# Sums of weight pieces made from DRAM to DRAM by copying and accumulating transfers, in a hybrid encoder layer

## The chip, the cores and the metric

The kernel runs on one core of a Trainium2 chip. The metric is the time of one execution in microseconds (us), measured on the device. A core has engines that run side by side: TensorE (PE in the profile; its weight loads are PEld), VectorE (DVE), ScalarE (ACT), GpSimd (POOL) and SyncE (SP). SP, ACT and POOL issue the transfers (DMA), which 16 DMA engines carry out.

## The reference, cut to what matters

One layer of an encoder with a model width of 1024 in float32, on 1056 frames in two request groups: 1024 of a prompt and 32 of a sample.

```python
h = rms_norm(x, g_mix); z = h @ w_in            # q, k, v, conv h/B/C, gates a/b: 50 columns of 128
a  = window_attention(q, k, v, sink) @ w_attn_out
bo = (cb * causal_conv3(cc * ch)) @ w_conv_out
x += (sigmoid(ga) * a + sigmoid(gb) * bo) @ w_mix_out
x += memory_attention(rms_norm(x, g_cross)) @ w_co
x += square(relu(rms_norm(x, g_mlp) @ w_up)) @ w_down       # 1024 -> 4096 -> 1024
y  = rms_norm(x, g_final)
```

The new keys and values, the last rows of the convolution and the memory keys and values are outputs too.

## The kernel before, in words

The 1056 frames lie in three chunks of 384, 384 and 288, with features on the partitions. Each matrix product is made from weight pieces of 128 x 1024 (512 KB). Every operand is split into a high part (cast on ACT, the helper's line L120) and a low part (the remainder, on DVE, L121), and each product is made of three matmuls: high x high, high x low, low x high.

Some products use fewer multiplications, by sums of operands (a Strassen-like scheme over 2 x 2 blocks): the *x pairs* (15 pairs of columns of w_in), the *up pairs* (12 pairs of columns of w_up) and the down product. They need sums of weight pieces as well as of activations. Where these are made is what the change is about:

- **Down.** For each of 8 (j, t) the four pieces s0..s3 of w_down give d3 = s2 + s3, d2 = s0 + s2, d0 = s0 + d3 and d1 = s1 + d0. The kernel before makes them on POOL, in 32 smaller steps: a load of 512 KB on POOL's own queue (L742), four additions of 128 x 256 (L749), a store of 512 KB into the DRAM tensor `wsum_d` (L750). The steps stand at chosen slots of the attention (13), in most x pairs (12) and, for the rest, among the last columns of w_in and the first of the attention's output. The down stage then loads w_sum pieces from `wsum_d` just as it loads w_down. In both tensors one 128 x 1024 piece is four runs of 256 numbers, so rows of 1 KB.
- **Pairs.** For columns r1 and r2 of a pair, halves a and b, `pair_sums` makes s31 = (r1a + r2a, r2a + r2b) and s24 = (r1a + s31b, r1b + s24a) from the two tiles in SBUF, 128 x 512 each: for an x pair two on DVE and two on POOL, for an up pair all four on POOL (L881 to L884). ACT and DVE split the result for the matmuls.

The stages follow each other in time: start with keys and values; 48 slots of attention units, with the projections of q, convolution and gates among them as other work; the start of the x pairs; the x pairs; the last columns of w_in and the attention's output; the convolution's output, mix and memory attention; the first columns of w_up; the up pairs; down; final norm. In each attention unit POOL normalises three of four heads (`S`, L579) with the reciprocal from DVE, ahead of TensorE's transposes (L589).

A scheduler orders the instructions of each engine from a simulation of their times, and `pin` keeps those that it is put around in the order of the program. A weight tile `wr` has two buffers. Loads of weights, activations and spilled tensors go on SP's queue, in order; POOL's transfers go on a queue of software descriptors.

In the start, the first weight is loaded in two halves on ACT's queue (L282, L283), behind the parameters, while SP loads the activations x0 in four parts (L290); TensorE runs 14 matmuls on a tile of ones (L328) before the data come.

## Time and profile before

| | us |
|---|---|
| median of 3 runs (lowest to highest) | 1767.47 (1766.37 to 1769.14) |
| the profiled execution | 1767.74 |
| its span, first to last instruction | 1766.0 |
| TensorE busy | 1733.7 |
| VectorE busy | 1213.3 |
| ScalarE busy | 846.1 |
| GpSimd busy | 657.9 |

The time of an execution is its span and 1.74 us around it. Busy time is time in which an engine carries out instructions; issuing of transfers does not count. The share of TensorE is 98% over the whole run, but what an edit is worth depends on the stage it is in, so the prediction goes by stages. In views of the trace a row `out<-in` names the tile written and the tile read, by the names of the program with their numbers left out.

### The profile page before, as it was taken

What the parts mean: (1) busy time and instruction counts of PE and PEld (TensorE: products, weight loads), DVE (VectorE), ACT (ScalarE), POOL (GpSimd) and SP (SyncE); (2) the same over time, 40 slices, a digit from 0 to 9 for tenths busy, and PEclk for the clock granted to TensorE, in tenths of its full rate; (3) what the DMA queues carried; (4) which work ended last, traced back from release to release, by engine and by line L of the source; (5) the groups of instructions that cost most, each with busy time, mean ns of one, the idle gap of its engine ahead of it and who ended that gap; (6) DMA issues with size and microseconds to landing.
All of it is one profiled execution on the core that took longest, in us unless ns stands there. A gap on an engine that the chain in (4) does not pass through costs nothing.

```text
span 1766.0 us, 30039 instructions
## 1 busy us (share of the span) xinstructions
PE 1733.7 (98%) x11008; PEld 1711.6 (97%) x11008; DVE 1213.3 (69%) x2130; ACT 846.1 (48%) x1625; POOL 657.9 (37%) x702
## 2 busy tenths in 40 slices
PE   8999999999999999999999999999999999999997
PEld 8999999999999999999999999999999999999997
DVE  6768888777887767367576877666666675445665
ACT  8667767852232245144465755642222353432553
POOL 2246675643744534402324241375544300100111
PEclk9999999999999999999999999999999999999998
DMA  5413434442322527789766767744443497544674
GB/s 183 146 58 106 141 114 147 139 153 98 132 86 96 177 102 263 261 255 320 259 218 208 242 219 240 253 166 155 130 139 124 149 316 221 176 152 141 230 240 134
DMA packets 178115, 313.01 MB, mean 177 GB/s; under 512 B 18192, under 2 KB 137776, under 8 KB 177840
## 3 DMA queue, kind: packets, MB, share of 16 engines
q1 hardware_dynamic: 168320, 276.97, 47.2%
q0 software_dynamic: 9216, 33.56, 5.4%
q8 instruction: 86, 1.41, 0.3%
q10 hardware_dynamic: 432, 0.58, 0.1%
q14 instruction: 61, 0.50, 0.1%
HBM read 233.23 MB, written 77.81 MB: 176 GB/s over the span
## 4 chain that ended last, share of the span: by engine, by line
PE 72%; DMA 9%; DVE 6%; ACT 5%; issue 3%; POOL 2%; SPq 1%; POOLq 0%; DVEq 0%; ACTq 0%
PE acc L176 7%; PE acc L178 7%; PE acc L177 7%; PE acc L892 7%; PE acc L894 7%; PE acc L893 7%; PE acc L1707 5%; PE acc L1706 5%; PE acc L1708 5%; PE pa L177 3%; PE pa L178 3%; PE pa L176 3%; DVE wl L121 2%; ACT wh L120 1%; PE pt L589 1%
## 5 line engine op out<-in xcount | busy, mean ns | idle before, releaser
L120 ACT CAST wh<-wr 128x1024 fp32r<-128x1024 f32 (+1 forms) x224 | 234.1, 1045 | 311.4 <-PE acc L1707 77.1
L121 DVE TENSOR_TENSOR wl<-wr,wh 128x1024 fp32r<-128x1024 f32 (+1 forms) x224 | 307.3, 1372 | 93.2 <-ACT wh L120 91.7
L176 PE MATMUL acc<-Y,wh 128*128 128x384 f32 (+1 forms) x624 | 201.9, 324 | 2.6 <-DVE ct L1081 1.5
L178 PE MATMUL acc<-Y,wl 128*128 128x384 f32 (+1 forms) x624 | 201.6, 323 | 0.3 <-DVE wl L121 0.3
L177 PE MATMUL acc<-Y,wh 128*128 128x384 f32 (+1 forms) x624 | 201.6, 324 | 0.0
L253 POOL TENSOR_TENSOR xacc<-xacc,ct 128x384 f32<-128x384 f32 (+1 forms) x62 | 78.0, 1257 | 322.2 <-ACT ct L251 319.8
L176 PE MATMUL acc<-X,wh 128*128 128x384 f32 (+1 forms) x528 | 172.6, 327 | 1.2 <-ACT wh L120 1.2
L177 PE MATMUL acc<-X,wh 128*128 128x384 f32 (+1 forms) x528 | 171.8, 325 | 0.9 <-DVE X L257 0.9
L178 PE MATMUL acc<-X,wl 128*128 128x384 f32 (+1 forms) x528 | 171.0, 324 | 0.0
L176 PEld LDWEIGHTS acc<-Y,wh 128*128 128x128 f32 x624 | 117.0, 188 | 3.9 <-DVE ct L1081 1.9
L178 PEld LDWEIGHTS acc<-Y,wl 128*128 128x128 f32 x624 | 117.2, 188 | 0.6 <-DVE wl L121 0.6
L177 PEld LDWEIGHTS acc<-Y,wh 128*128 128x128 f32 x624 | 117.1, 188 | 0.0
L579 POOL TENSOR_SCALAR S<-S,rec 128x256 f32<-128x256 f32 (+1 forms) x96 | 93.3, 984 | 62.1 <-DVE rec L576 61.9
L1706 PE MATMUL acc<-Y,wh 128*128 128x384 f32 (+1 forms) x352 | 113.1, 321 | 0.2 <-ACT Y L120 0.2
L1707 PE MATMUL acc<-Y,wh 128*128 128x384 f32 (+1 forms) x352 | 113.1, 321 | 0.1
L1708 PE MATMUL acc<-Y,wl 128*128 128x384 f32 (+1 forms) x352 | 112.9, 321 | 0.0
L120 ACT CAST wh<-s 128x1024 fp32r<-128x1024 f32 x54 | 56.6, 1051 | 105.9 <-PE acc L893 72.3
L177 PEld LDWEIGHTS acc<-X,wh 128*128 128x128 f32 x528 | 100.0, 189 | 2.9 <-DVE X L257 1.8
L176 PEld LDWEIGHTS acc<-X,wh 128*128 128x128 f32 x528 | 99.8, 189 | 2.2 <-ACT wh L120 1.4
L178 PEld LDWEIGHTS acc<-X,wl 128*128 128x128 f32 x528 | 99.8, 189 | 1.0 <-DVE wl L121 0.2
L121 DVE TENSOR_TENSOR Y<-ct,Y 128x384 fp32r<-128x384 f32 (+1 forms) x128 | 68.9, 570 | 28.7 <-ACT Y L120 28.5
L120 ACT CAST Y<-ct 128x384 fp32r<-128x384 f32 (+1 forms) x128 | 59.2, 486 | 60.0 <-DMA ct<-bc_d 14.8
(405 smaller groups left out, 5360.3 us busy)
## 6 DMA issues: line engine op xcount, KB each, us to landing
wr<-in_w_in SPq DMA_DIRECT2D x55, 512.0 KB, 3.6
wr<-in_w_up SPq DMA_DIRECT2D x48, 512.0 KB, 3.8
wr<-in_w_down SPq DMA_DIRECT2D x32, 512.0 KB, 4.0
wr<-wsum_d SPq DMA_DIRECT2D x32, 512.0 KB, 3.5
wl<-wl_d SPq DMA_DIRECT2D x28, 512.0 KB, 4.8
wr<-in_w_conv_out SPq DMA_DIRECT2D x24, 512.0 KB, 4.5
wr<-in_w_mix SPq DMA_DIRECT2D x24, 512.0 KB, 4.7
xacc<-in_w_down POOLq DMA_DIRECT2D x21, 512.0 KB, 3.9
```

The costliest lines, as they stand in the source:

```text
L120: act.copy(hi, src)
L121: dve.tensor_sub(lo, src, hi.bitcast(F32))
L176: pe.matmul(out, wh[:, a], hi, start=(k == 0), stop=False)
L177: pe.matmul(out, wh[:, a], lo, start=False, stop=False)
L178: pe.matmul(out, wl[:, a], hi, start=False, stop=(k == len(acts) - 1))
L579: pool_e.tensor_scalar_mul(stl[:, h, :nk], stl[:, h, :nk], rec[:, h : h + 1])
L892: pe.matmul(acc, wh[:, a], hi, start=(start and k == 0), stop=False, skip_group_check=True)
L893: pe.matmul(acc, wh[:, a], lo, start=False, stop=False, skip_group_check=True)
L894: pe.matmul(acc, wl[:, a], hi, start=False, stop=(k == 3), skip_group_check=True)
L1706: pe.matmul(a, wh[:, s], hi, start=(start and k == 0), stop=False, skip_group_check=True)
L1707: pe.matmul(a, wh[:, s], lo, start=False, stop=False, skip_group_check=True)
L1708: pe.matmul(a, wl[:, s], hi, start=False, stop=(stop and k == len(acts) - 1), skip_group_check=True)
```

## The change

Three parts.

**1. Down sums.** The pieces of w_down are laid out on the host as [q, j, t, 128, 1024], so that each is one block with rows of 4 KB, and `wsum_d` becomes four tensors of the same shape. Nothing of the sums passes through SBUF any more. For each (j, t), SP issues four DRAM-to-DRAM copies of 512 KB (d3 from s3, d2 from s0, d0 from s0, d1 from s1), and POOL issues five accumulating transfers of 512 KB in three phases: d3 += s2 and d2 += s2; d0 += d3 and d1 += d3; d1 += s0. One copy goes out in each attention slot from slot 2 (32 in all), one add in each from slot 8 (40 in all), with the phases of three (j, t) interleaved. The buffer `ws` and POOL's additions are gone.

**2. Up sums.** The same for the up pairs, two at a time, into four DRAM tensors `usum_d`: 24 copies on SP (three in each x pair from the second) and 30 adds on POOL (up to four in each x pair from the third). In the up stage each pair loads s31 and s24 with four transfers of 256 KB on SP, right behind the loads of the pair's own columns; `pair_sums` is left to the x pairs.

**3. Start.** The halves of the first weight are issued by SP, behind the first and second part of x0; the matmuls on ones become 18.

```diff
-    wsum_d = dram.tile([4, 2, 4, P, 4, 256], F32, name="wsum_d")
+    usum_d = [[dram.tile([12, P, 512], F32, name=f"us{k}{h}_d") for h in "ab"] for k in ("31", "24")]
+    wsum_d = [dram.tile([4, 2, P, 1024], F32, name=f"wsum_d{q}") for q in range(4)]
...
-            act.dma_start(raw[:, halves[0]], weight(worder[0])[:, halves[0]])
-            act.dma_start(raw[:, halves[1]], weight(worder[0])[:, halves[1]])
+            return [lambda h=h: sp.dma_start(raw[:, h], weight(worder[0])[:, h]) for h in halves]
...
                     sp.dma_start(raw[:, 2 * h : 2 * h + 2], io[f"x{c}"][:, 2 * h : 2 * h + 2])
+                    if first:
+                        first.pop(0)()
...
-        for _ in range(14):
+        for _ in range(18):
...
-            for to, x, y in ((3, 2, 3), (2, 0, 2), (0, 0, 3), (1, 1, 0)):
-                pin(pool_e.tensor_tensor(t[:, to], t[:, x], t[:, y], op=ALU.add))
-            pin(pool_e.dma_start(wsum_d[at], t))
...
+    def sum_parts(j, t):
+        s = [io["w_down"][q, j, t] for q in range(4)]
+        d = [wsum_d[q][j, t] for q in range(4)]
+        copies = [lambda to=to, x=x: pin(sp.dma_start(to, x)) for to, x in ((d[3], s[3]), (d[2], s[0]), (d[0], s[0]), (d[1], s[1]))]
+
+        def add(to, x):
+            return lambda: pin(pool_e.dma_start(to, x, accum_op=ALU.add, max_dma_last_dim=4096))
+
+        return copies, [[add(d[3], s[2]), add(d[2], s[2])], [add(d[0], d[3]), add(d[1], d[3])], [add(d[1], s[0])]]
+
+    sums = [sum_parts(j, t) for j in range(4) for t in range(2)]
+    copies = [x for c, _ in sums for x in c]
+    adds = [x for s in range(len(sums) + 2) for ph in (2, 1, 0) if 0 <= s - ph < len(sums) for x in sums[s - ph][1][ph]]
...
+    for i, x in enumerate(copies):
+        at(2 + i, x)
+    for i, x in enumerate(adds):
+        at(8 + i, x)
...
-        side = dve if key[0] == "x" else pool_e
-        side.tensor_tensor(s31[:, b], r2[:, a], r2[:, b], op=ALU.add)
+        dve.tensor_tensor(s31[:, b], r2[:, a], r2[:, b], op=ALU.add)
...
+        return [copy(s31b, r2b), copy(s31a, r1a), copy(s24a, r1a), copy(s24b, r1b)], [
+            [add(s31b, r2a), add(s31a, r2a)], [add(s24a, s31b), add(s24b, s31b)], [add(s24b, r1a)]
+        ]
...
+            if i and what in ("W1", "W4", "W3"):
+                for x in ucopies[:1]:
+                    ucopies.pop(0)()
+            if i > 1 and what in ("B11", "H", "W1", "W2"):
+                for x in uadds[:1]:
+                    uadds.pop(0)()
...
+    def up_sums(i):
+        if i >= len(UP):
+            return
+        for two, tag in zip(usum_d, ("s31", "s24")):
+            t = PW["pool"].tile([P, 1024], F32, tag=tag, name=nm(tag))
+            for h in range(2):
+                sp.dma_start(t[:, 512 * h : 512 * h + 512], two[h][i])
+            raws["u", i].append(t)
```

How the change stands in the order of the engines. First POOL in the attention, before: `xacc` and `ws` hold pieces of w_down, `S` are scores.

```order
L742 DMA xacc_2304<-in_w_down 128x1024
L749 TENSOR_TENSOR ws_2079<-ws_2079 128x256
L563 COPY S_2416<-nsink 128x4
L749 TENSOR_TENSOR ws_2079<-ws_2079 128x256 x3
L750 DMA wsum_d<-ws_2079 128x1024
L579 TENSOR_SCALAR S_2416<-S_2416,rec_2428 128x256 x3
L563 COPY S_2505<-nsink 128x4
```

The same place now; a transfer into `wsum_d` on POOL is an accumulating one:

```order
L737 DMA wsum_d_102<-in_w_down 128x1024
L737 DMA wsum_d_101<-wsum_d_104 128x1024
L578 TENSOR_SCALAR S_2425<-S_2425,rec_2437 128x256 x3
L737 DMA wsum_d_102<-wsum_d_104 128x1024
L562 COPY S_2516<-nsink 128x4
```

The load, the four additions and the store are gone, and single adds stand between the normalisations of the scores.

Then SP at the first stores of the attention's output (`m_d`), before: `ct` on the right are products, `wr` weights.

```order
L1082 DMA m_d_83<-ct_8400 128x384
L138 DMA wr_8623<-in_w_attn_out 128x1024
L1082 DMA m_d_84<-ct_8435 128x384
L1082 DMA m_d_83<-ct_8469 128x384
L1082 DMA m_d_84<-ct_8502 128x384
L1082 DMA m_d_85<-ct_8530 128x288
```

Now, with loads of x (`xt`) and of the memory keys (`mkr`):

```order
L1157 DMA xt_9560<-in_x 128x384
L1090 DMA m_d_83<-ct_8321 128x384
L1157 DMA xt_9602<-in_x 128x384
L1157 DMA xt_9644<-in_x 128x384
L1172 DMA mkr_9935<-mk_d 64x256 x2
L1090 DMA m_d_84<-ct_8349 128x384
L138 DMA wr_8532<-in_w_attn_out 128x1024
L1090 DMA m_d_83<-ct_8383 128x384
L1172 DMA mkr_9942<-mk_d 64x256 x2
```

The loads of x and of the keys, which came some 15 rows further down, stand among the first stores.

Last, POOL at the second up pair, before: `s` are the pair's sums, `xacc` the square of a half, `ct` a partial sum.

```order
L1424 TENSOR_TENSOR xacc_9241<-xacc_9241 128x384
L881 TENSOR_TENSOR s_2746_14009<-wr_2714_13769 128x512
L884 TENSOR_TENSOR s_2746_14009<-wr_13768,wr_2714_13769 128x512
L1356 TENSOR_TENSOR ct_13961<-ct_13959 128x288
L882 TENSOR_TENSOR s_2747_14010<-wr_13768,s_2746_14009 128x512
L1424 TENSOR_TENSOR xacc_9241<-xacc_9241 128x384
L883 TENSOR_TENSOR s_2747_14010<-wr_13768,s_2747_14010 128x512
```

Now:

```order
L1392 TENSOR_TENSOR Y_2665_13597<-lt_13575,Y_2664_13596 128x384
L1363 TENSOR_TENSOR ct_13875<-ct_13873 128x288
L1363 TENSOR_TENSOR ct_13920<-ct_13918 128x288
L1440 TENSOR_TENSOR xacc_9149<-xacc_9149 128x384
L1487 TENSOR_TENSOR lt_13988<-xacc_9149,lt_13988 128x384
```

The sums are gone from POOL; the rows around them follow each other directly.

More of the change, by code (lines that the diff above doesn't have):

```diff
@@ L126, in weight @@
             q, j, t = at
-            return (wsum_d if name == "w_sum" else io[name])[j, t, :, :, q].rearrange("i p c -> p i c")
+            return wsum_d[q][j, t] if name == "w_sum" else io[name][q, j, t]
         src = io[name]
@@ L136, in fetch_w @@
         raw = wp.tile([P, 1024], F32, tag="wr", bufs=2, name=nm("wr"))
[L137 to L138 removed]
+        sp.dma_start(raw, weight(worder[wpos[0] + len(fetched)]))
         fetched.append(raw)
@@ L326, in norm_x @@
         turn = ps.tile([P, P], F32, tag="pt", bufs=2, name=nm("pt"))
-        for _ in range(14):
+        for _ in range(18):
             pe.matmul(turn, ones_r, ones_r, start=True, stop=True)
-        load_w()
+        first = load_w()
         with tc.manual_schedule(engines={mybir.EngineType.SP}):
-            load_x()
+            load_x(first)
         w_half = first_w()
@@ L729, in at @@
         events.setdefault(slot, []).append(fn)
-    W = {}
-    pieces = [(j, t, i) for j in range(4) for t in range(2) for i in range(4)]
-    def sum_load(acc):
-        W["acc"] = acc
-        if pieces:
-            at = pieces.pop(0)
-            if acc:
-                t = xacc_tile()[:, :1024].rearrange("p (q c) -> p q c", q=4)
-            else:
-                t = W["pool"].tile([P, 4, 256], F32, tag="ws", name=nm("ws"))
-            pin(pool_e.dma_start(t, io["w_down"][at]))
-            W["new"] = at, t
-    def sum_add(old):
-        if old:
-            at, t = old
-            for to, x, y in ((3, 2, 3), (2, 0, 2), (0, 0, 3), (1, 1, 0)):
-                pin(pool_e.tensor_tensor(t[:, to], t[:, x], t[:, y], op=ALU.add))
-            pin(pool_e.dma_start(wsum_d[at], t))
-    def sum_step():
-        old = W.pop("new", None)
-        sum_load(not W.get("acc", True))
-        sum_add(old)
-    def sum_done():
-        sum_add(W.pop("new", None))
+    def sum_parts(j, t):
[8 more added lines that the diff above has]
+    adds = [x for s in range(len(sums) + 2) for ph in (2, 1, 0) if 0 <= s - ph < len(sums) for x in sums[s - ph][1][ph]]
     for kv, starts in enumerate([(0, 1, 2, 4, 5, 6, 8, 9, 10)] * 3 + [(0, 1, 2, 3, 4, 5, 6, 7, 8)]):
@@ L879, in pair_sums @@
         s24 = PW["pool"].tile([P, 1024], F32, tag="s24", name=nm("s24"))
-        side = dve if key[0] == "x" else pool_e
-        side.tensor_tensor(s31[:, b], r2[:, a], r2[:, b], op=ALU.add)
+        dve.tensor_tensor(s31[:, b], r2[:, a], r2[:, b], op=ALU.add)
         pool_e.tensor_tensor(s24[:, a], r1[:, a], s31[:, b], op=ALU.add)
         pool_e.tensor_tensor(s24[:, b], r1[:, b], s24[:, a], op=ALU.add)
-        side.tensor_tensor(s31[:, a], r1[:, a], r2[:, a], op=ALU.add)
+        dve.tensor_tensor(s31[:, a], r1[:, a], r2[:, a], op=ALU.add)
         raws[key] += [s31, s24]
@@ L905, in hybrid_step, with up_sum_parts, copy, add @@
     LATE = 3
+    def up_sum_parts(at):
+        g, i = at // 4 + 1, at % 4
+        r1, r2 = (io["w_up"][8 * g + i + e : 8 * g + i + e + 2] for e in (0, 4))
+        a, b = slice(0, 512), slice(512, 1024)
+        r1a, r1b, r2a, r2b = r1[:, :, a], r1[:, :, b], r2[:, :, a], r2[:, :, b]
+        (s31a, s31b), (s24a, s24b) = [[t[at : at + 2] for t in two] for two in usum_d]
+        flat = lambda t: t.rearrange("i p c -> (i p) c")
+        def copy(to, x):
+            return lambda: pin(sp.dma_start(flat(to), flat(x)))
+        def add(to, x):
+            return lambda: pin(pool_e.dma_start(flat(to), flat(x), accum_op=ALU.add, max_dma_last_dim=2048))
+        return [copy(s31b, r2b), copy(s31a, r1a), copy(s24a, r1a), copy(s24b, r1b)], [
+            [add(s31b, r2a), add(s31a, r2a)], [add(s24a, s31b), add(s24b, s31b)], [add(s24b, r1a)]
+        ]
+    usums = [up_sum_parts(at) for at in range(0, 12, 2)]
+    ucopies = [x for c, _ in usums for x in c]
+    uadds = [x for s in range(len(usums) + 2) for ph in (2, 1, 0) if 0 <= s - ph < len(usums) for x in usums[s - ph][1][ph]]
     xs1, xemit = {}, {}
@@ L993, in after @@
         def after(what):
-            if what == "B11":
-                sum_done()
             todo.get(what, lambda: None)()
-            if what == "W3" and (i % 5):
-                sum_load(True)
+            if i and what in ("W1", "W4", "W3"):
[4 more added lines that the diff above has]
+                    uadds.pop(0)()
             if what == "B11" and XP[i][0][0] == "a" and "cv_cm" in S:
@@ L1087, in do_attn_out @@
         return fn
+    item(lambda: [x() for x in ucopies + uadds])
     item(open_y)
@@ L1105, in hybrid_step @@
     run()
-    assert not pieces and "new" not in W
     todo.extend((bcp, bc_d, 1, k) for k in range(NF))
-    closed(W["cm"])
     closed(x_cm)
@@ L1620, in up_start @@
         up_issue(0, 3)
+        up_sums(1)
         A = up_p1(1)
```

28 lines of the change are left out of this document (10 added, 18 removed).

## The prediction

> **What bounds the kernel now.** I read the page's busy shares first, then the span cut by stages, then what TensorE waits for, then the chain of waits around the two waits that the change touches.
>
> The busy shares, share of the span and number of instructions:
>
> ```profile
> PE 1733.7 (98%) x11008; PEld 1711.6 (97%) x11008; DVE 1213.3 (69%) x2130; ACT 846.1 (48%) x1625; POOL 657.9 (37%) x702
> ```
>
> TensorE is busy 98% of the span. The change neither adds nor removes a matmul of the layer, so it can only win from the 1766.0 − 1733.7 = 32.3 us in which TensorE stands still, and it loses whatever it adds to them. The stages show where they lie. Columns: from and to, length, then busy us and instructions of each engine, granted TensorE clock, busy share of the 16 DMA engines, GB/s:
>
> ```profile
> 0.00:17.00 17.00, 11.34 (x51) 9.43 (x52) 10.87 (x17) 13.81 (x27) 4.25 (x10) 1.00 0.89 309
> 88.00:354.00 266.00, 265.93 (x1757) 257.90 (x1756) 210.94 (x576) 195.29 (x499) 168.43 (x228) 1.00 0.35 117
> 410.00:662.00 252.00, 252.00 (x1569) 252.00 (x1568) 189.68 (x255) 78.61 (x103) 119.55 (x131) 1.00 0.35 120
> 662.00:750.00 88.00, 86.31 (x545) 85.67 (x544) 51.79 (x71) 31.85 (x52) 39.19 (x51) 1.00 0.77 261
> 750.00:1165.00 415.00, 406.33 (x2572) 400.35 (x2572) 292.77 (x508) 232.33 (x434) 124.01 (x112) 1.00 0.74 249
> 1165.00:1400.00 235.00, 232.90 (x1457) 231.95 (x1456) 145.03 (x185) 62.70 (x81) 127.24 (x104) 1.00 0.40 132
> 1400.00:1501.00 101.00, 99.86 (x635) 98.34 (x634) 71.28 (x128) 44.08 (x82) 5.12 (x5) 1.00 0.78 254
> ```
>
> The attention slots (88 to 354) and the x pairs (410 to 662), where most of the old sums are made, have no idle TensorE at all: 0.07 and 0.00 us. There POOL's arithmetic is free, and removing it wins nothing. Idle time that the change can reach is the 1.69 us of attention's output (662 to 750), some of the 2.1 us of the up pairs (1165 to 1400), and the 1.14 us at the start of the down stage (1400 to 1501). TensorE's waits by line, us in total, times, longest:
>
> ```profile
> PE acc L176 <- DVE ct L1081: 1.5, 1, 1.5
> PE acc L892 <- ACT wh L120: 1.3, 1, 1.3
> PE acc L1708 <- DVE wl L121: 0.8, 1, 0.8
> PE acc L892 <- ACT s L1417: 0.2, 1, 0.2
> ```
>
> The first row is the idle time of 662 to 750; the second and the last lie between 1165 and 1185; the third is at 1472.
>
> **Attention's output (last pieces of the down sums, moved away).** The chain around 707 us (start, us, what), and the transfers of 686 to 710 (count, KB each, median us to landing; first two rows by queue: packets, MB, share of 16 engines):
>
> ```profile
> 698.34 6.28 DMA ct<-ao_d
> 706.09 1.90 DVE Y L121 x2
> 708.08 0.57 DVE ct L1081
> ```
>
> ```profile
> q1 hardware_dynamic: 3255, 5.68, 70.5%
> q0 software_dynamic: 576, 2.10, 23.8%
> ct<-ao_d SPq DMA_DIRECT2D x9, 192.0 KB, 6.1
> ws<-in_w_down POOLq DMA_DIRECT2D x1, 512.0 KB, 7.5
> ```
>
> DVE's last conversions of attention rows wait for a load that takes 6.28 us; DVE then does them before the product with the gate (ct, L1081) that frees an accumulator for TensorE. POOL's queue takes 23.8% of the DMA engines just then, all of it pieces of the down sums. Over the whole run the same 192 KB load takes less:
>
> ```profile
> ct<-ao_d SPq DMA_DIRECT2D x16, 192.0 KB, 4.4
> ```
>
> After the change these pieces are long done (their adds go out one per attention slot) and the last adds for the up weights leave POOL ahead of this stage. 94% busy engines (70.5 + 23.8) fall to about 70%, the load saves up to 6.28 − 4.4 = 1.9 us, and the 1.5 us wait goes with it. I take the whole idle time of the stage, **−1.7 us**. Its bounds: −1.7 (no more is idle here), and 0 if another load takes the place: the order hoists loads of the cross-attention keys and gates into these rows of SP's queue, among the output stores.
>
> **The up pairs' sums (48 POOL additions removed, 48 loads of 256 KB added).** The costliest of the four groups of additions in this stage (count, busy, mean ns, idle before), then the chain around 1181 us:
>
> ```profile
> L882 POOL TENSOR_TENSOR s<-wr,s 128x512 f32<-128x512 f32 x11 | 20.4, 1853 | 0.0
> ```
>
> ```profile
> 1174.67 1.25 POOL s L881
> 1175.92 1.25 POOL s L884
> 1177.79 1.24 POOL s L882
> 1179.78 1.28 POOL s L883
> 1181.09 1.05 ACT wh L120
> 1182.18 0.44 PE acc L892
> ```
>
> Four additions in a row, the cast of their result, and only then the matmul: this is the 1.3 us wait. With the sums loaded, the cast waits only for loads that the order puts ahead of the pair's first product. In the other pairs the additions (1.85 us each in the row above) are hidden: TensorE's products run on behind them, and of the 2.1 us idle in the whole stage only 2.1 − 1.5 = 0.6 are left for all of them. So the gain is 1.3 + 0.2 = **−1.5 us**, bounds −2.1 (all idle time of the stage) and 0 (the loads come late: 24 times 512 KB more in 235 us, at the 1.5 us of all engines worked out below, lift the DMA share from 0.40 to about 0.55).
>
> **Down weights in 4 KB rows.** The start of the down stage waits for a chain of transfers; its last member:
>
> ```profile
> 1475.96 4.05 DMA ct<-hid_d
> ```
>
> The row above for this stage has a DMA share of 0.78. Pieces of 1 KB become rows of 4 KB in the 64 weight loads of this stage. What rows of 4 KB are worth is seen only indirectly (KB, median us to landing):
>
> ```profile
> wr<-in_w_up SPq DMA_DIRECT2D x48, 512.0 KB, 3.8
> wr<-in_w_down SPq DMA_DIRECT2D x32, 512.0 KB, 4.0
> wr<-wsum_d SPq DMA_DIRECT2D x32, 512.0 KB, 3.5
> ```
>
> w_up has the 4 KB rows already, the others 1 KB pieces: no clear difference. The bounds are −1.1, all that is idle there, and 0; with no nearer row I take the middle, **−0.5 us**. The Trainium skill, page "DMA: Bandwidth & Descriptors", section "Specifications", gives 512 B as the smallest transfer for line rate; by it the term is 0, and the sum 3.2 us instead of 3.7. The three rows agree with it better than with a gain.
>
> **What is added in the attention and the x pairs.** 56 copies on SP's queue and 70 accumulating transfers on POOL's, 512 KB each. No row of before shows either. The nearest are POOL's own transfers of 512 KB, and the time they take of the 16 engines:
>
> ```profile
> q0 software_dynamic: 9216, 33.56, 5.4%
> xacc<-in_w_down POOLq DMA_DIRECT2D x21, 512.0 KB, 3.9
> wsum_d<-xacc POOLq DMA_DIRECT2D x21, 512.0 KB, 3.1
> ```
>
> 64 transfers take 5.4% of 1766, 95 us, so 1.5 us of all engines each. I take 1.5 for a copy (a load that ends elsewhere) and 1.5 to 3.0 for an add (one source read, or two). Attention, where 13 of the 32 old pieces lie: 32 × 1.5 + 40 × (1.5 to 3.0), less 26 old transfers × 1.5, is 69 to 129 us in the 282 of the attention slots; the share rises from 0.35 to 0.6 to 0.8. X pairs, with 12 old pieces: 24 × 1.5 + 30 × (1.5 to 3.0), less 24 × 1.5, is 45 to 90 in 252: 0.35 to 0.53 to 0.71. The stage from 750 to 1165 runs at 0.74, and its TensorE stands still 2%. The work in these two stages is cast and split well ahead, and TensorE is idle for 0.07 us in both together. POOL keeps in attention only the normalisation of the scores ahead of TensorE's transposes, and waits for it more than it works late:
>
> ```profile
> POOL S L579 <- DVE rec L576: 61.9, 23, 16.2
> ```
>
> That is a spare of 61.9/23 = 2.7 us each time, and the removed additions add to it. An add that needs an earlier add waits on POOL with the next normalisation behind it, but it goes out at least two slots after it, 2 × 5.9 us (the 48 slots fill this stage and some 16 us of the next, 282/48). Landing would have to exceed 11.8 us; load and store in a row take 3.9 + 3.1 = 7.0. I take **0**, bounds 0 and +10 (below). The 25 old pieces whose additions leave these stages win nothing, since nothing is idle there.
>
> **The start.** The first weight's halves go to SP's queue between the activations, and four warm-ups are added. The chain there:
>
> ```profile
> 4.86 0.61 ACT X L256
> 11.84 0.95 ACT wh L120
> 12.82 2.04 DVE wl L121
> 14.90 0.38 PE acc L188
> ```
>
> From 4.86 to 12.8 ACT works through its list; TensorE's last wait ends behind the split of the second weight. Bytes and their total are the same at 309 GB/s, so I take **0**; bounds −1 and +1 (an x part one transfer later).
>
> **Sum.** −1.7 − 1.5 − 0.5 + 0 + 0 = −3.7 us on the profiled execution, 1767.74 → 1764.0. That execution is 0.27 above the median of the runs, 1767.47, so I forecast **1763.8 us**. Its own range by the bounds of the four small terms is 1762 to 1768.
>
> **Rivals.**
> *The accumulates are slow, and POOL stands in their way (slower).* One mechanism: an add that waits for an earlier one holds POOL, the normalisation behind it is late, and TensorE's transposes (pt, L589) or the first x pair wait. It decides once an add lands after 11.8 + 2.7 = 14.5 us, twice the 7.0 above. Against it: the spacing. For it: transfers on busy engines do take twice as long (7.5 for a load of 3.9, rows above). At 16.5 us some 7 of the 40 adds would each cost 2 us: +14 − 3.7, or about 1777; at 15 us, 0.5 × 10 − 3.7: 1769. I price it at **1772**, chance 0.20. The Trainium skill, same page, section "Issuing engines are not separate DMA queues", says that transfers share the same 16 engines whichever engine starts them; the trace agrees, with SP's load at 6.1 beside POOL's at 7.5 in the window above, so moving sums off POOL does not take their bytes off SP's loads.
>
> *The stalls refill (same).* At 707 us the hoisted loads of keys and gates fill the place of the sums, so −1.7 falls away, or the sums' loads of the up pairs come late. Sum −2.0: **1765.5**, chance 0.33. For it: 64 KB keys took a place in SP's queue among the stores, and 70.5% of the engines stay busy; against it: they are small.
>
> *More is won (faster still).* With POOL's arithmetic gone, DVE and ACT run their splits earlier, and the whole idle time of 1400 to 1501 and part of the 8.7 us of 750 to 1165 go: −3.7 − 0.6 − 2.5, **1760.7**, chance 0.12. Against it: the POOL work that leaves lies before 750 and after 1165.
>
> **How the numbers follow.** The forecast has 0.35. A measurement of this kernel tells 0.2%, 3.5 us, from no change; the forecast lies just beyond it, at −3.7. Faster: most of the forecast's 0.35 that lies beyond −3.5 (0.22), the 0.12, and 0.08 for gains at several unpriced places, together 0.44; same: the 0.33 and the rest of the forecast, less what the tails take, 0.37; slower 0.19. The range that holds 8 in 10 leaves a tenth on each side: **1759 to 1774**.
>
> **What would show it.** The wait on ct L1081 near 707 us gone, and with it the ct<-ao_d landing near 4.4; no POOL s rows between 1165 and 1400, and no wait on wh L120 near 1181; POOL waiting for an accumulate less than 3 us at a time; no TensorE wait on L589 or L891-L893 new in attention or the x pairs. Wrong would be: DMA shares above 0.9 in attention, landing times of adds beyond 12 us, or a new wait in the first x pair.

## The result, and the profile after

The changed kernel takes **1793.82 us** (median of 4 runs, 1792.94 to 1800.18), the kernel before 1767.14 in the same comparison: a ratio of 1.0147, 95% interval 1.0131 to 1.0163. The forecast was 1763.8. It is 26.7 us slower, and outside the range of 1759 to 1774.

The profiled execution took 1793.94 us with a span of 1792.1. Its busy shares, and its stages cut at the same places of the work (some 10 to 27 us later on the clock than before):

```profile
PE 1741.6 (97%) x11012; PEld 1718.5 (96%) x11012; DVE 1166.2 (65%) x2130; ACT 844.0 (47%) x1625; POOL 491.3 (27%) x532
```

```profile
88.00:354.00 266.00, 264.02 (x1741) 255.99 (x1740) 202.60 (x572) 194.21 (x495) 139.99 (x186) 1.00 0.76 196
354.00:420.00 66.00, 60.99 (x375) 59.97 (x374) 45.33 (x66) 32.23 (x59) 25.20 (x25) 0.97 0.69 177
432.00:697.30 265.30, 249.08 (x1499) 246.65 (x1498) 161.53 (x244) 75.27 (x100) 86.74 (x96) 0.97 0.67 158
1180.00:1420.00 240.00, 238.47 (x1508) 237.91 (x1507) 138.41 (x191) 67.32 (x90) 71.56 (x64) 1.00 0.59 187
1420.00:1520.00 100.00, 97.93 (x620) 96.59 (x619) 70.83 (x128) 40.83 (x77) 5.07 (x5) 1.00 0.78 257
```

The third row holds 1499 matmuls of the x pairs. The same 1499 before:

```profile
426.90:668.00 241.10, 241.10 (x1499) 241.10 (x1498) 181.75 (x244) 76.82 (x100) 116.12 (x128) 1.00 0.34 115
```

So 24.2 us of the 26.7 are lost here: 16.2 in which TensorE stands still (265.3 − 249.1), and 8.0 because the same matmuls take longer (249.1 − 241.1). Up to 6.8 of these 8.0 come from the granted clock, 0.97 on average where it was 1.00 (worked out under "The clock" below). What TensorE waits for in this stretch now (before: nothing):

```profile
PE acc L877 <- DVE lt L980: 8.5, 3, 4.3
PE acc L877 <- DVE lt L972: 6.1, 3, 4.1
PE acc L877 <- ACT s L942: 1.6, 2, 1.1
```

These are the instructions with which DVE and ACT read a pair's products; they free the accumulators. They are late because POOL is. POOL's groups of accumulating transfers in this stretch, with the idle time of POOL just ahead of each (after the bar: busy us, mean ns, idle us and what ended it; on POOL the 0.9 us of issuing counts as busy):

```profile
L903 POOL DMA_DIRECT2D us31a_d<-in_w_up x6 | 5.4, 906 | 14.8 <-issue 14.8
L903 POOL DMA_DIRECT2D us24a_d<-us31b_d x6 | 5.4, 898 | 24.5 <-issue 24.5
L903 POOL DMA_DIRECT2D us24b_d<-in_w_up x6 | 5.4, 898 | 30.3 <-issue 27.4 <-DVE lt L980 3.0
L903 POOL DMA_DIRECT2D us24b_d<-us31b_d x6 | 5.4, 896 | 27.3 <-issue 27.3
L903 POOL DMA_DIRECT2D us31b_d<-in_w_up x5 | 4.5, 899 | 16.7 <-issue 8.2 <-DVE lt L966 5.5 <-DVE lt L973 3.0
```

POOL stands for 14.8 + 24.5 + 30.3 + 27.3 + 16.7 = 113.6 us ahead of 29 adds, and 102.2 of it are "issue": time in which it waits for nothing that the profile shows. One such place, first POOL, then ACT, DVE and TensorE behind it (start us, us, instruction, in brackets the idle time before it):

```profile
486.01 0.90 POOL L903 DMA_DIRECT2D us24b_d<-in_w_up  x1 [10.61 <-issue]
486.57 0.45 POOL L618 MEMSET u<- 128x2 f32 x1
486.61 1.18 POOL L619 COPY u<-prm 128x2 f32<-128x2 f32 x1
494.78 0.89 POOL L903 DMA_DIRECT2D us24a_d<-us31b_d  x1 [6.99 <-issue]
495.36 1.61 POOL L867 TENSOR_TENSOR s<-wr,s 128x512 f32<-128x512 f32 x1
497.05 1.29 POOL L868 TENSOR_TENSOR s<-wr,s 128x512 f32<-128x512 f32 x1
```

```profile
498.37 1.04 ACT L121 CAST wh<-s 128x1024 fp32r<-128x1024 f32 x1 [12.03 <-POOL s L868]
```

```profile
499.45 1.23 DVE L122 TENSOR_TENSOR wl<-s,wh 128x1024 fp32r<-128x1024 f32 x1 [10.33 <-ACT wh L121]
500.59 0.55 DVE L980 TENSOR_TENSOR lt<-acc,lt 128x384 f32<-128x384 f32 x1
```

```profile
501.29 0.42 PE L877 MATMUL acc<-tk,wh 128*128 128x384 f32 x1 [3.17 <-DVE lt L980]
```

Two adds hold POOL for 10.6 and 7.0 us, and the sums for the next x pair (L867, L868) stand behind them. ACT's cast waits 12 us for these sums and DVE's remainder 10 us for the cast. The instruction behind it on DVE, which frees the accumulator, is late with it, and TensorE stands for 3.2 us.

To see where time goes from stage to stage I matched the two executions matmul by matmul and took how much later each one starts (us; minus is earlier). The first column is the time in the kernel before; three kernels of the experiments below stand beside the change. Each column is one profiled execution.

```
at (before)                        change   down alone   4 KB rows   adds in x pairs
  23  start done                    -0.3       +0.1        +0.1          -0.5
 303  attention, most of it         -1.1       -0.8        -0.4          -1.7
 387  attention done                +0.4       +0.4        -1.3          -1.9
 407  x start done                  +5.1       +6.3        +3.9          +0.5
 688  x pairs done                 +29.2       +6.3        +3.9          +0.5
 749  attention's output            +27.0       +4.0        +1.6          -1.9
1132  memory attention done        +26.3       +1.9        -1.7          -4.4
1243  first up pairs               +26.9       +2.0        -0.7          -4.1
1705  down, most of it             +26.5       +3.2        +1.0          -3.6
```

The change loses 24.1 in the x pairs, 4.7 at the x start and 1.5 at the end of the attention, and gains 2.2 at the attention's output.

### The profile page after: what moved, and what is told of

Its sections match the earlier page's. It is cut to its first block, busy times and chain, and to the rows that moved or that the text cites. A ratio compares the mean times of both kernels' runs of the same rounds, so it can differ in the third digit from the quotient of the medians.

```text
span 1792.1 us, 30070 instructions
## 1 busy us (share of the span) xinstructions
PE 1741.6 (97%) x11012; PEld 1718.5 (96%) x11012; DVE 1166.2 (65%) x2130; ACT 844.0 (47%) x1625; POOL 491.3 (27%) x532
## 3 DMA queue, kind: packets, MB, share of 16 engines
q0 software_dynamic: 13920, 36.70, 12.5%
## 4 chain that ended last, share of the span: by engine, by line
PE 49%; DMA 5%; DVE 4%; ACT 2%; issue 1%; POOL 0%; SPq 0%; POOLq 0%; DVEq 0%; ACTq 0%
PE acc L176 5%; PE acc L177 5%; PE acc L178 5%; PE acc L1726 5%; PE acc L1724 5%; PE acc L1725 5%; PE acc L877 4%; PE acc L879 4%; PE acc L878 4%; DMA ct<-bc_d 2%; PE pa L177 1%; PE pa L176 1%; PE pa L178 1%; DVE wl L122 1%; DMA ct<-b_d 1%
## 5 line engine op out<-in xcount | busy, mean ns | idle before, releaser
L121 ACT CAST wh<-wr 128x1024 fp32r<-128x1024 f32 (+1 forms) x224 | 234.2, 1045 | 290.6 <-PE acc L1725 84.1
L122 DVE TENSOR_TENSOR wl<-wr,wh 128x1024 fp32r<-128x1024 f32 (+1 forms) x224 | 290.9, 1298 | 95.3 <-ACT wh L121 94.2
L121 ACT CAST wh<-s 128x1024 fp32r<-128x1024 f32 x54 | 56.2, 1049 | 126.6 <-PE acc L878 62.0
L122 DVE TENSOR_TENSOR wl<-s,wh 128x1024 fp32r<-128x1024 f32 x54 | 70.0, 1296 | 42.7 <-ACT wh L121 42.7
L877 PE MATMUL acc<-X,wh 128*128 128x384 f32 x240 | 82.4, 343 | 12.0 <-DVE lt L972 6.1
```

The lines of the kernel that those rows point to most:

```text
L121: act.copy(hi, src)
L122: dve.tensor_sub(lo, src, hi.bitcast(F32))
L877: pe.matmul(acc, wh[:, a], hi, start=(start and k == 0), stop=False, skip_group_check=True)
```

## The experiments

**Which part, and waits or traffic.** Four kernels. First the down sums alone: part 2 undone.

```diff
-        dve.tensor_tensor(s31[:, b], r2[:, a], r2[:, b], op=ALU.add)
+        side = dve if key[0] == "x" else pool_e
+        side.tensor_tensor(s31[:, b], r2[:, a], r2[:, b], op=ALU.add)
...
-    ucopies = [x for c, _ in usums for x in c]
+    ucopies = []
...
+    uadds = []
```

> The change without part 2: the up pairs' sums stay on POOL, the down sums and the start as changed. Two theories of the loss in the x pairs (24 us of the 26.7): W, waits: an add on POOL waits, in order, for its copy on SP's queue, which lands late, and POOL's sums and convolution rows for the x pairs stand behind it; T, traffic: copies and adds keep the DMA engines busy and every load and store lands late. Both put the loss on part 2, since the down sums' transfers end with the attention. Expected by both: the stretch of the x pairs as before (0, not +24), and the loss of 1.5 us at the end of attention and of 4.4 us at the x start left: 1767.1 - 0.8 (start) + 1.5 + 4.4 - 2.1 (attention's output) = 1770, within 3.

Measured: 1770.67 us, ratio 1.0010 (1.0000 to 1.0019). The x pairs lose nothing; the x start loses 5.9.

Then the up sums alone: in the changed kernel, the old code for the down sums (load, four additions, store on POOL) put back.

> The change without part 1: the down sums as before on POOL with loads and stores (and 1 KB rows), the up sums by copies and adds, and the start as changed. W and T both: no loss at the end of attention and at the x start, 20 us or more lost in the x pairs (POOL has the down pieces there as well, 24 transfers more and 36 us of arithmetic): 1787 to 1800. If the time is below 1775, the loss needs both parts together, by a third way.

Measured: 1808.02 us, ratio 1.0219 (1.0204 to 1.0235). 36 us lost in the x pairs, nothing at the end of the attention and at the x start. The loss in the x pairs belongs to part 2, that at the x start to part 1.

Then the adds moved three pairs behind their copies:

```diff
-            if i > 1 and what in ("B11", "H", "W1", "W2"):
+            if i > 4 and what in ("B11", "H", "W1", "W2"):
```

> The change with the up adds starting three x pairs later (from pair 5, not from pair 2); copies, bytes and number of transfers are the same, only the distance between a copy and its add grows from a fraction of a pair to three pairs (some 50 us). W: no add waits for a copy any more, the stretch of the x pairs loses 0 to 6 us instead of 24: 1770 to 1776. T: the same bytes in nearly the same stretch, loss of 18 to 24: 1788 to 1794.

Measured: 1794.07 us, ratio 1.0136 (1.0121 to 1.0151). Still 21.5 us lost in the x pairs: theory W falls. The trace shows something else. From some place on every add goes out just after the one before has landed (worked out from the trace's issue and landing times, us):

```
us31a_d  issued 614.92  landed 621.86
us24b_d  issued 622.17  landed 628.56
us24a_d  issued 628.88  landed 635.54
us24b_d  issued 635.85  landed 642.41
us31b_d  issued 642.73  landed 648.51
us31a_d  issued 648.83  landed 654.77
```

0.31 us after each landing, also where the two adds touch different tensors (us24b_d and us31b_d), and with no wait of the program between them. The changed kernel shows the same: 21 of its 29 steps from one up add to the next are of this kind.

And each up add cut to 32 of its 256 rows, which leaves most of the up sums out:

```diff
-            return lambda: pin(pool_e.dma_start(flat(to), flat(x), accum_op=ALU.add, max_dma_last_dim=2048))
+            return lambda: pin(pool_e.dma_start(flat(to)[:32], flat(x)[:32], accum_op=ALU.add, max_dma_last_dim=2048))
```

> The change with each up add cut to an eighth (32 of 256 rows, so most of the up sums are left out), in the same order on every engine and with the same waits; the copies are whole. The adds take about 3.2 us of all DMA engines each now (12.5% of 1792 us over 70), 40% of the engines in the x pairs, and would take 0.4. W in the form that the copies are late by themselves: the adds still wait for copies, loss of 15 us or more: 1785 to 1794. T: the share of the DMA engines in the x pairs falls from 0.73 to about 0.4 and the loss to 0 to 6 us: 1770 to 1776. In between: the copies are late because the adds take the engines, a chain of both.

Measured: 1770.94 us, ratio 1.0016 (1.0005 to 1.0027); 0 lost in the x pairs. This fits T, but also any theory in which adds with many rows hold POOL: here adds of 32 rows overlap, and POOL idles 5 us ahead of them.

**The ring.** The profile names SP's queue `hardware_dynamic` and POOL's `software_dynamic`. The next theory, R, is that POOL has to find room for the descriptors of a transfer's rows before it can go on; then the number of rows in flight sets how many adds overlap. The queue's packets give the rows of each transfer, changed kernel first, then the next experiment:

```profile
q0 software_dynamic: 13920, 36.70, 12.5%
```

```profile
q0 software_dynamic: 10080, 36.70, 11.5%
```

13920 is 40 × 144 + 30 × 272 packets: 128 rows and 16 more for each down add, 256 and 16 for each up add. 10080 is 70 × 144: up adds of 128 rows of 4 KB, which need the up weights in two halves on the host.

```diff
-        flat = lambda t: t.rearrange("i p c -> (i p) c")
+        flat = lambda t: t.rearrange("i (p o) c -> (i p) (o c)", o=2)
...
-    a["w_up"] = _cols(i["w_up"][0])
+    a["w_up"] = _cols(i["w_up"][0]).reshape(32, P, 2, 512).transpose(2, 0, 1, 3)
```

> The whole change with the up weights laid out on the host in two halves, so that each up copy and add has 128 rows of 4 KB and not 256 rows of 2 KB; bytes and transfers are the same, and the up columns are loaded in rows of 2 KB. After the first runs theory W (adds wait for late copies) fell, since three pairs of lag changed nothing. New rival to T: R, the ring. In the x pairs each add of 256 rows goes out 0.31 us after the one before has landed, 15 times and more in a row, with no wait of the program between; the adds of 128 rows for the down sums overlap (issued up to 10 us before the one ahead lands). So POOL stands still in each add for want of room for its descriptors, and POOL's sums for the x pairs stand behind it. R: no add issued at the landing of the one before, POOL not held, x pairs lose 0 to 6 us: 1770 to 1777. T, only the engines' time counts: the same 24 us lost, 1787 to 1795.

Measured: 1771.72 us, ratio 1.0023 (1.0009 to 1.0037). The x pairs lose **0**, with the same bytes on POOL's queue (36.70 MB above) and nearly as many busy DMA engines as in the changed kernel (0.65 against 0.67). Its stage of the x pairs, and POOL's idle time ahead of the same five groups there:

```profile
420.00:670.00 250.00, 250.00 (x1554) 250.00 (x1553) 188.02 (x251) 79.11 (x102) 90.45 (x97) 1.00 0.65 178
```

```profile
L904 POOL DMA_DIRECT2D us24b_d<-in_w_up x6 | 6.2, 1036 | 0.3 <-DMA us24b_d<-us31b_d 0.3
L904 POOL DMA_DIRECT2D us31a_d<-in_w_up x6 | 5.9, 990 | 0.1
L904 POOL DMA_DIRECT2D us24a_d<-us31b_d x6 | 5.2, 874 | 4.4 <-DMA us31b_d<-in_w_up 3.2 <-DVE wl L122 1.3
L904 POOL DMA_DIRECT2D us31b_d<-in_w_up x6 | 5.2, 871 | 2.6 <-DVE wl L122 2.3 <-issue 0.4
L904 POOL DMA_DIRECT2D us24b_d<-us31b_d x6 | 5.2, 868 | 6.4 <-issue 2.2 <-DVE ct L680 2.1 <-DVE lt L973 2.1
```

113.6 us have become 13.8. T, with traffic alone, falls: it asked for 1787 or more. The landings themselves are longer here than in the changed kernel (medians of 6.9 to 11.6 us for the five groups, where it had 6.2 to 6.6), since the adds now run beside each other, and nobody waits for them.

The other cut of an add, all 256 rows with 64 of 512 numbers, which leaves out as much of the sums:

```diff
-            return lambda: pin(pool_e.dma_start(flat(to), flat(x), accum_op=ALU.add, max_dma_last_dim=2048))
+            return lambda: pin(pool_e.dma_start(flat(to)[:, :64], flat(x)[:, :64], accum_op=ALU.add, max_dma_last_dim=2048))
```

> The whole change with each up add cut to an eighth in the other direction: 256 rows of 64 numbers (256 B) and not of 512, so most of the up sums are left out; order and waits are those of the change. R, if the number of descriptors counts: the adds still go out one after another, 0.31 us after the landing of the one before, and POOL is held, though for shorter if they land sooner: 1772 to 1785. T: the engines are free of the adds, as with the adds of 32 rows (1770.9): 1769 to 1773, and adds overlap.

Measured: 1773.84 us, ratio 1.0040 (1.0025 to 1.0056). The bytes are the eighth of before, as with the 32 rows, yet the adds run one after the other again, and POOL idles 59.8 us ahead of them. They land in about 3 us, so the single holds are short: the x pairs lose 3.3.

Last, rows of 2 KB but 128 to a transfer: each up add issued as two.

```diff
+                for r in (slice(0, P), slice(P, 2 * P)):
+                    pin(pool_e.dma_start(flat(to)[r], flat(x)[r], accum_op=ALU.add, max_dma_last_dim=2048))
```

> The whole change as it is, each up add issued as two of 128 rows of 2 KB (256 KB each) in place of one of 256 rows. If the number of rows in flight sets the limit: the two halves overlap, up to three of 128 rows are in flight as in the attention, POOL is held for a shorter time, and the x pairs lose 2 to 14 us: 1772 to 1784. If it is the length of a row (2 KB against 4 KB): every half goes out 0.31 us after the landing of the one before, and the loss is 24 us or more: 1792 to 1805.

Measured: 1776.24 us, ratio 1.0060 (1.0040 to 1.0081). Halves overlap: when one is issued it is the third in flight in 38 of 60 cases and never the fourth. It is the number of rows that counts, not their length. POOL idles 49.5 us, and the x pairs lose 6.6.

So 128 rows are not free of the hold either; it only begins later. With three adds of 128 rows in flight the next one goes out 0.3 us after the first of them lands. POOL in the kernel with 28 down adds in the attention (below), where landings came at 601.35, 604.40 and 607.35 us:

```profile
601.66 0.81 POOL L904 DMA_DIRECT2D us24b_d<-us31b_d  x1 [1.60 <-issue]
604.70 0.81 POOL L904 DMA_DIRECT2D us31b_d<-in_w_up  x1 [2.23 <-issue]
607.66 0.81 POOL L904 DMA_DIRECT2D us31a_d<-in_w_up  x1 [2.15 <-issue]
```

Over the kernels with up sums by transfers, POOL's idle time ahead of the up adds and the loss in the x pairs (us):

```
kernel                          rows per add     POOL idle   lost in the x pairs
change                          256 of 2 KB        113.6          24.1
three pairs of lag              256 of 2 KB        110.7          21.5
up alone                        256 of 2 KB         99.7          36.5
thin adds                       256 of 256 B        59.8           3.3
split adds                      2 x 128 of 2 KB     49.5           6.6
up alone, 4 KB rows             128 of 4 KB         16.8           3.0
4 KB rows                       128 of 4 KB         13.8           0.0
small adds                       32 of 2 KB          5.0           0.0
```

The idle time here is all that lies ahead of the adds, whatever ended it (with three pairs of lag up to 700 us; a few adds go out later); in the 4 KB kernel 2.6 of the 13.8 us are "issue". The loss does not grow in step with it: 59.8 us of short holds cost 3.3.

**The up sums alone with 4 KB rows**, and the traffic as a cause of its own.

> The up sums alone with rows of 4 KB, the down sums as before on POOL. With rows of 2 KB the same kernel took 1808, 36 us of it lost in the x pairs. R: adds of 128 rows beside POOL's loads and stores of 128 rows fit together, and the loss in the x pairs falls from 36 to 0 to 8 us: 1764 to 1776. T (bytes on the engines, 0.80 of them there): no better than 1795.

Measured: 1774.40 us, ratio 1.0033 (1.0021 to 1.0045), where 2 KB rows gave 1808.02. The x pairs lose 3.0 with a DMA share of 0.77; another 4.4 are lost at the start of the down stage.

**The x start.** In the changed kernel SP's stores beside the late down adds take three to five times as long. Transfers of 340 to 372 us, changed kernel, then before (count, KB, median us to landing):

```profile
sg_d<-ct SPq DMA_DIRECT2D x4, 192.0 KB, 6.7
ao_d<-AO SPq DMA_DIRECT2D x4, 128.0 KB, 9.1
```

```profile
sg_d<-ct SPq DMA_DIRECT2D x4, 192.0 KB, 1.9
ao_d<-AO SPq DMA_DIRECT2D x4, 128.0 KB, 1.8
```

The eight loads of x behind them go out at 373.4 us and not at 369.2, and TensorE then stands once, for 4.3 us, for a cast (L121). So the down adds were packed to end earlier, first with the up sums on POOL:

```diff
-        at(8 + i, x)
+        at(6 + i * 33 // 39, x)
```

> The kernel with the down sums alone (up sums on POOL), its 40 adds packed into slots 6 to 39 of the attention and not 8 to 47. In the kernel with the down sums alone the x start is 6 us late, and there the stores of SP ahead of the x start land after 8 to 11 us where they took 1.8 before, while four adds are in flight from 348 to 370 us; the loads of x for the pairs then go out at 373 and not at 369. If these late adds are the cause: no loss at the x start, 1764 to 1767. If the loss stays, it comes from the order of SP or POOL at that place: 1769 to 1772.

Measured: 1768.81 us, ratio 1.0007 (0.9992 to 1.0021). The x start is clean (+0.4), but the attention loses 10 us in the profiled execution, which took 1774.30 us, 5.5 more than the median:

```profile
88.00:354.00 266.00, 259.10 (x1693) 251.13 (x1692) 194.85 (x550) 186.64 (x478) 138.95 (x185) 0.98 0.79 204
```

A miss in the total. The late adds were the cause at the x start, but here nearly all of the 10 us come from one place: SP's loads of x for the x pairs' sums (`KSh`) land after 11.1 us from 281 on, ACT and DVE stand behind them, and TensorE stops for 5.4 us at 290 and has a granted clock of 0.50 for 10.2 us around it. The busy engines alone do not explain it, as the same packing with 4 KB rows shows:

> Both edits on the whole change: up adds of 128 rows of 4 KB, and the down adds packed into slots 6 to 39. R and the late adds together: 1764 to 1769, the size of the forecast; under T alone no better than 1783.

Measured: 1771.61 us, ratio 1.0019 (1.0007 to 1.0031), a miss: nothing gained over 4 KB rows alone. At a DMA share of 0.80 the same loads land after 6.3 us; the attention loses 0.4 up to 303 us and then 2.2; the x start is clean (+0.1), and 3.3 go at the start of the down stage.

Each down add cut to 16 of its 128 rows, which leaves most of the down sums out, with the 4 KB rows for the up sums:

```diff
-            return lambda: pin(pool_e.dma_start(to, x, accum_op=ALU.add, max_dma_last_dim=4096))
+            return lambda: pin(pool_e.dma_start(to[:16], x[:16], accum_op=ALU.add, max_dma_last_dim=4096))
```

> The change with 4 KB rows for the up adds (1771.7), with each down add cut to 16 of its 128 rows, so most of the down sums are left out; copies whole, order nearly the same. If the adds' traffic beside SP's stores makes the x start late: the 5 us there fall to 0 to 1, 1765 to 1768. If it is the order at the x start: 4 to 5 us stay, 1770 to 1772. The kernel with all adds in the x pairs kept 2.4 of them, so half and half is the likeliest.

Measured: 1771.71 us, ratio 1.0025 (1.0012 to 1.0039). The x start loses 1.9 and not 5.2: some 3.3 of its loss go with the adds' rows and bytes (this cut takes both away, so it does not tell traffic from holds of POOL), and the rest is there without them; that the changed order makes it is argued. That the total did not fall comes, in this profiled execution, from the start of the down stage, where it loses 4.3.

**Other places for the down adds.** All 40 moved into the x pairs, three to a pair, and the up sums on POOL:

```diff
-    for i, x in enumerate(adds):
-        at(8 + i, x)
...
+    uadds = list(adds)
...
-            if i > 1 and what in ("B11", "H", "W1", "W2"):
+            if i and what in ("B11", "W1", "W2"):
```

> The down sums alone (up sums on POOL), with the 32 copies in the attention as changed and all 40 adds moved into the x pairs, three to a pair. The adds of 128 rows overlap, so by R they do not hold POOL there. What is left of the loss with the adds in the attention (0 to 2 us at its end, 4 to 6 at the x start) is put down to stores and loads of SP that land late beside the adds. If so: attention and x start as before, x pairs as before, the gain of 2.1 at the attention's output kept: 1763 to 1767. If the copies or the order alone make the x start late: 1768 to 1772. If 128-row adds hold POOL in the x pairs too: above 1772.

Measured: 1765.71 us, ratio **0.9987** (0.9974 to 1.0000). Its median is the only one of this study below the kernel before; its interval reaches 1, as those of four other kernels here do, so it is not shown to be faster. Its profiled execution, the fastest of its ten: attention −1.9, x start +2.4, x pairs 0, attention's output −2.3. Its stage of the attention runs at half the DMA share of the change:

```profile
88.00:354.00 266.00, 265.87 (x1757) 258.33 (x1756) 205.56 (x575) 195.46 (x498) 112.62 (x150) 1.00 0.40 129
```

And with 4 KB rows for the up sums, 28 down adds in the attention and 12 in the x pairs, or 15 and 25:

> The whole change with 4 KB rows, 28 of the 40 down adds in slots 8 to 35 of the attention, so that none is in flight near the x start, and the other 12 at the head of the up adds in the x pairs, four to a pair. If late adds delay the x start and 128-row adds cost the x pairs nothing: the 5 us of the x start come back, 1764 to 1768. If the x pairs start to lose with the DMA share at about 0.8, T has a part: 1769 to 1780.

> As the one before, with only 15 down adds in the attention, in every second slot from 8 to 36, and 25 in the x pairs before the up adds, from the second pair on: about 55 adds of 3 us in 250 us there. By R alone 1763 to 1768, since the attention has fewer transfers than with 28; if a DMA share near 0.95 holds the loads of weights and the spills, several us are lost in the x pairs: 1770 to 1785.

Measured: 1769.06 us, ratio 1.0007 (0.9995 to 1.0019), and 1770.62 us, ratio 1.0010 (0.9999 to 1.0020). The x pairs lose 1.7 and 1.1 us at DMA shares of 0.77 and 0.87:

```profile
420.00:670.00 250.00, 249.22 (x1543) 248.31 (x1542) 190.94 (x249) 78.92 (x102) 100.08 (x109) 1.00 0.77 201
```

```profile
420.00:670.00 250.00, 249.42 (x1545) 248.96 (x1544) 186.66 (x249) 78.84 (x102) 105.09 (x117) 1.00 0.87 222
```

POOL is still held in both: it idles 34 and 39 us ahead of the up adds there. So the 1.7 and 1.1 us are what traffic and holds cost together, and a share of 0.87 by itself costs no more than that. What holds the first of the two above the expected 1768 is the x start, where 2.9 of the 5 us stayed; the second loses 2.9 there too and 3.6 at the start of the down stage.

## Why the prediction was wrong

**The step that failed** is "What is added in the attention and the x pairs", and in it the sentence that reckons with a hold of POOL only for an add that "needs an earlier add". The price of 0, with a bound of +10, rested on spacing and on landing times. Both were about right: the median add landed after 8.3 us in the attention and 6.3 in the x pairs, below the 11.8 us that were allowed (two of 70 took 13.0 and 13.1), and three pairs of spacing changed nothing. What the step lacked is that an accumulating transfer can be held on POOL by the rows of those in flight, whatever it depends on: two adds of 256 rows were never in flight together, and POOL stood up to 10.6 us for one, where the prediction's sign of being right was less than 3. It cost 24.1 us. The prediction counted transfers and bytes and never rows, though part 2 has 256 rows of 2 KB to a transfer and part 1 128 rows of 4 KB. For its price it looked at what stands behind an add in the attention alone; in the x pairs that is the pair's own two sums on POOL. That the rows count is shown by the cuts and splits above; that it is room for their descriptors is the likeliest reason, and no trace shows it.

The Trainium skill, page "DMA: Bandwidth & Descriptors", section "SWDGE vs HWDGE vs iDMA", says that a DMA of GpSimd is built by GpSimd itself, which appends descriptors to rings that the DMA engines drain. The trace agrees as far as it goes: it is POOL that stands still, 113.6 us ahead of its own transfers; no run shows the rings themselves.

**The rival "the accumulates are slow, and POOL stands in their way"** had the right engine and the right consequence (POOL's normal work stands behind an add), with 0.20, but the wrong condition (an add that waits for an earlier one, landing after 14.5 us), the wrong place (the attention and the first x pair) and less than a fifth of the price: 1772 against 1793.8.

**The cost of an add** on the engines was taken as 1.5 to 3.0 us; it is 12.5% of 1792 us over 70, 3.2 on average. The DMA share of the attention was forecast to be 0.6 to 0.8 and is 0.76, that of the x pairs 0.53 to 0.71 and is 0.67. The shares were right; that traffic at such shares costs the x pairs next to nothing was right too (0 with 4 KB rows). At the end of the attention and at the x start it was wrong: 1.5 and 4.7 us. In the 4 KB kernel the x start loses 5.2, and 1.9 when the down adds are cut to 16 rows. "TensorE is idle for 0.07 us in both together" showed that the stage had no stall, not how much slack it had: stores of 1.8 us could take some more, but not 9.

**Attention's output, −1.7.** The size was right, the reason was not: the wait is gone, and the matched matmuls gain 2.2 us between 688 and 749. But the kernel with the up sums alone (4 KB rows) gains 2.2 there too, and it still makes the down pieces at that place. Its transfers of 686 to 716 us:

```profile
q0 software_dynamic: 846, 3.07, 27.8%
ct<-ao_d SPq DMA_DIRECT2D x9, 192.0 KB, 6.0
ws<-in_w_down POOLq DMA_DIRECT2D x2, 512.0 KB, 6.8
```

```profile
670.00:760.00 90.00, 90.00 (x574) 89.82 (x573) 51.27 (x72) 31.70 (x52) 35.57 (x48) 1.00 0.78 270
```

The pieces' queue takes 27.8% (23.8 before), the load of attention rows 6.0 us (6.1 before), and TensorE does not stop. So the traffic of the pieces was not what stopped it, and that the size came out is luck. What these kernels share is a changed order of the loads and conversions around it; that the order is the cause is argued, not shown. The hoisted loads of keys and gates took nothing back. Of the rival "more is won" a part came true: from 749 to 1132 us the change gains 0.7, the 4 KB kernel 3.3 and the one with the adds in the x pairs 2.5, where the sum had nothing; the cause is open.

**The up pairs, −1.5.** The four additions are gone, but a new wait took their place. TensorE's waits from 1155 to 1220 in the changed kernel:

```profile
PE acc L877 <- ACT wh L121: 0.9, 1, 0.9
PE acc L877 <- DVE lt L1465: 0.6, 1, 0.6
PE acc L176 <- DVE ct L1356: 0.4, 1, 0.4
PE acc L176 <- ACT wh L121: 0.3, 1, 0.3
```

The first is the cast of the first pair's own column: SP issued its load only at 1178.68 us, it landed at 1184.57, and ACT took it at once. From 1132 to 1243 the balance is +0.6, not −1.5. Here the rival "the stalls refill" was right, in another place than it named.

**Down in rows of 4 KB, −0.5.** Measured −0.4 in the changed kernel between 1404 and 1504, but −0.6 to +5.2 at the same place in the kernels of the experiments, so it is not shown to be a gain, and that −0.4 lies so near −0.5 is luck. The stage start still ends in one wait:

```profile
PE acc L1726 <- DVE wl L122: 1.3, 1, 1.3
```

The losses there do not go with the rows of the weights: the two largest, 5.2 and 4.4, are those of the kernels with the up sums alone, which keep the 1 KB pieces. They go with the clock. In the seven kernels whose profiled execution has a granted clock of 0.50 for 3.4 us at this place they are 2.0 to 5.2, in the others −0.6 to 2.4. What makes TensorE's wait longer there is open.

**The start, 0.** −0.6 to +0.9 in the profiled executions of the kernels with this part: as forecast.

**The clock** was not in the prediction at all. A stop of TensorE can cost more than its length. Three windows of 10 us around the three long stops of the x pairs (4.1, 3.2 and 4.3 us), and one that follows the last:

```profile
462.00:472.00 10.00, 6.62 (x24) 6.62 (x25) 6.13 (x9) 3.54 (x5) 4.91 (x8) 0.66 0.71 112
496.00:506.00 10.00, 6.83 (x31) 6.54 (x30) 6.52 (x10) 3.31 (x4) 3.15 (x3) 0.83 0.82 154
568.00:578.00 10.00, 5.69 (x24) 5.40 (x23) 6.66 (x10) 3.31 (x4) 3.00 (x3) 0.83 0.82 157
578.00:588.00 10.00, 10.00 (x66) 10.00 (x65) 6.50 (x12) 2.73 (x3) 4.92 (x7) 1.00 0.59 142
```

The granted clock is 0.66, 0.83 and 0.83 there, and 1.00 where TensorE has been busy for a while. The trace has it at 0.50 for 6.8, 3.4 and 3.4 us, which is what 0.66 and 0.83 over 10 us come to. These 13.7 us at half speed cost at most 6.8 of the 8.0 us above; the rest is not accounted for. How long a stop has to be is not settled by these runs: a stop of 1.9 us at the end of the attention, near 353 us, has a clock of 0.50 for 3.4 us behind it in the kernel with three pairs of lag, and 1.00 in the changed kernel. The Trainium skill, page "TensorE: Matmul & The Clock Gate", section "HAM oscillation — how this bites in real kernels", gives as its rule that TensorE should have no idle gaps of over some 3.4 us; the traces do not bear that length out, since the clock also fell beside stops of 3.2 and 1.9 us.

**Sums of the prediction.** The chance of "faster" is given as 0.44, and its parts, 0.22 + 0.12 + 0.08, make 0.42. The price of 16.5 us landings, +14 − 3.7 on 1767.5, is 1778 and not 1777. Neither changes the forecast.

**What stays open.** How many rows the software queue takes exactly: three adds of 128 rows were in flight and never four, and never two of 256, but in the kernel with the up sums alone in 4 KB rows a fourth transfer was in flight in three cases, with a load or a store of a down piece among the four. Which moved instruction makes the 1.9 to 2.4 us of the x start that stay without the late adds. And why the 4 KB kernel's median lies 4.0 us above the kernel before, when its profiled execution is only 1.9 above it.

## What to carry to other kernels

Count the rows of a transfer on POOL's queue, not only its bytes: POOL both computes and issues transfers, and here a transfer with many rows held its arithmetic until an earlier one had landed, where the same bytes in half as many, longer rows cost the x pairs nothing. An engine that is busy only 27% of the time can still be the one that everything waits for, if its order is fixed and one of its instructions can block; look at what stands behind the new instruction, not at the engine's busy share. And in a kernel bound by TensorE a stop can be dearer than its length: 16.2 us of stops came with 8.0 us of slower matmuls.

## What the runs showed that was not expected

- Adds of 256 rows on POOL's queue ran strictly one after another, the next at the earliest 0.31 us after the landing of the one before; adds of 128 rows ran up to three at a time. No wait of the program stands between them, and the profile calls POOL's idle time "issue".
- An accumulating transfer of 512 KB from DRAM to DRAM took 3.2 us of all 16 engines on average and landed after 5.1 to 13.1 us, where POOL's transfers of 512 KB between DRAM and SBUF took 1.5 on average and a load landed after 3.9.
- With up to three adds in flight and a DMA share of 0.65 to 0.87, TensorE's x pairs lost 0 to 1.7 us (3.0 with POOL's loads and stores of down pieces among the adds). In the attention a share of 0.79 went with a loss of 10 us in one profiled execution and one of 0.80 with 2.2 in another; at 0.76 to 0.77, in seven others, the matched matmuls came out between 0.9 earlier and 3.0 later from 303 to 387 us.
- TensorE's granted clock fell to 0.50 beside stops as short as 1.5 us (at the start of the down stage, in the kernel with early adds and 4 KB rows), always for 3.4 us or more.
